# GpSimd operations of a hybrid decoder layer cut into pieces of 256 columns, and the border into the feed-forward stage regrouped

## The chip, the core and the metric

One Trainium2 chip, one of its cores. The metric is device time of one execution in microseconds (us), the median of several runs. PE is TensorE (matrix multiply; PEld is its weight load), DVE is VectorE, ACT is ScalarE, POOL is GpSimd and SP is SyncE, which issues the DMAs. SBUF is the memory on the chip from which the engines read, and PSUM the one into which TensorE writes.

## The reference

One layer, one step: a prompt of 1024 tokens and 8 single-token samples, 1024 channels, weights in float32.

```python
def layer(x, ...):
    y = mixer_block(rmsnorm(x, norm_mix_g), ...)
    x = x + y
    x = x + cross_attn(rmsnorm(x, norm_x_g), mk, mv, w_xq, w_xo)
    x = x + swiglu(rmsnorm(x, norm_ffn_g), w_gate, w_up, w_down)
...
def mixer_block(h, ...):
    proj = h @ w_in                                  # everything below is cut from proj
    rq, rk = rotary(rq, pos), rotary(rk, pos) * RET_DK ** -0.5      # 4 heads of 128
    o_r = retention_chunked(rq, rk, rv, state)       # scores, state update, chunk by chunk
    y_a = (silu(rg) * groupnorm(o_r)) @ w_branch_a
    gq, gk, gv = silu(causal_conv(qkv, 4 taps))      # 8 heads of 128
    o_g = gated_delta_chunked(l2norm(gq), l2norm(gk), gv, beta, g, state)
    y_b = (rmsnorm(o_g) * silu(z)) @ w_branch_b
    return (sigmoid(ga) * y_a + sigmoid(gb) * y_b) @ w_out
def rotary(x, pos):                                  # the rotation
    return concat([x1 * cos - x2 * sin, x1 * sin + x2 * cos])
def swiglu(h, w_gate, w_up, w_down):
    return (silu(h @ w_gate) * (h @ w_up)) @ w_down
```

## The kernel before

Every operand of a large product is split into a high part (rounded, written by ScalarE) and a low part (the rest, by one subtraction), and each product is three matmuls: high by high, high by low, low by high. `wsplit` (L245 to L255) does it for a weight tile of 128x1024: a DMA brings `wf`, ScalarE writes `wh`, and `wl = wf - wh` is written by the engine in `wlo[0]`: GpSimd in the gated-delta stage, else VectorE (L254). TensorE reads `wl` last of the three.

The stages follow each other in time, counted from the start of the span: the start (to 50 us); the gated-delta stage, in which the chains of 8 heads run beside the dense products of the input projection (50 to 950); retention, with the samples' single steps beside it (950 to about 1170); the branch products, keys and values and `w_out` (to 1490); cross-attention (to 1690); its output projection with the residual in two halves of 516 columns, the border (1690 to 1870); pairs of feed-forward column blocks (to 2260); the down projection.

On TensorE the order is written by hand in the gated-delta and retention stages; on the other engines a scheduler sets it from its own estimate of when data arrive, and each engine then works through its list in order.

In the gated-delta stage VectorE runs the four-tap convolution (`cyq`, `cyk`, `cyv`, L526, 1056 columns, both inputs in SBUF), the evacuations of the projection (`ev`, L361, input in PSUM; L365, both in SBUF) and the small steps of the recurrence (`R` L764, `S` L780). GpSimd runs `wl` (60 times) and 128x512 operations, 16 of each: `A` (L629), `dg` (L633), `qe` (L659), `U` and `Tm` (L725), `os` (L797), `ol` (L799), `oT` (L813).

In retention `ret_qk` rotates queries and keys of one unit (a head and half of the tokens, 8 units): `swapped` (L887) writes `rsw` in two operations of 64x1024 that read the other half of the partitions, then `rqk` is multiplied (L904) and added to (L905), 128x1024 each, all on GpSimd. `svn` (L1151, L1152) and `qS` (L1156, L1189) are the samples' delta-rule steps on VectorE; TensorE reads `svn`. `kv` (L1268) evacuates keys and values of the memory; TensorE waits for its bank. `b0l` to `b7l` (L236) are low parts of the gated-delta output, and `rS_0l` (L236) that of the retention state, which TensorE reads.

The border. `residual_half(c, ms)` runs `w_xo` tile by tile for token half c and adds the residual into `xr` (L1558); the squares are summed on GpSimd (L1563), and `rsnorm` (L310 to L319) turns the sum into the factor `rsB`: a logarithm (L315) and an exponential (L317) on ScalarE for each of two blocks of columns. `scale(r, c)` (L1571) multiplies 128x1032 tiles of `xr` by `rsB`; `operands(p, ...)` splits the operand of product p into `xop_0` to `xop_3`. Each pair of weight blocks (`w_gate`, `w_up`) needs seven products, as in Strassen's scheme; the sums of weights that products 5, 6, 7 and 3 need (`S1`, `S2`, `wu`) are formed on GpSimd (L1687) when `weights(p)` first asks for them, and a product (24 matmuls of 258 columns) then splits its weights into `wp_f` (L235, L236). `preload_act_table_set` puts a set of functions that holds both logarithm and exponential into ScalarE; an `ACT_TABLE_LOAD` changes the set.

Of the kernel before, what the change touches and what calls it, by code (L numbers as in the profile page):

```python
# [17 lines left out]
P = 128  # L18
# [4 lines left out]
KT = D // P  # L23
# [120 lines left out]
def build(tc, io):  # L144
# [21 lines left out]
    with ExitStack() as es:  # L166
# [73 lines left out]

        wlo = [ve]
# [379 lines left out]
        def gdn_decay(h, u):  # L621

            n = f"{h}_{u}"
            hc = slice(4 * u, 4 * u + 4)
            A = gtile("A", f"A{n}", 2)
            qe = gtile("qe", f"qe{n}", 4)
            dg = gtile("dg", f"dg{n}", 4)
            dma(out=qe, in_=gr_d[h * NCH + 4 * u:h * NCH + 4 * u + 4].rearrange("c t -> (c t)").partition_broadcast(P))
            ge.tensor_tensor(v4(A), v4(qe), bcol(gcum[:, h, hc]), op=ALU.subtract)  # L629
            se.activation(A, A, AF.Abs)  # L630
            se.activation(A, A, AF.Exp, scale=-1.0)
            se.activation(qe, qe, AF.Exp)
            ge.tensor_tensor(v4(dg), v4(A), bc(triu), op=ALU.mult)  # L633
            return qe, dg, A
# [80 lines left out]
        def gdn_inverses(h, units, U32):  # L715
# [7 lines left out]
            for u in range(2):  # L723
                for dst, src in ((Us[u], U32), (Tm[u], T32)):
                    ge.tensor_tensor(dst.rearrange("p (c b i) -> p c b i", c=4, b=4), src[:, 4 * u:4 * u + 4].unsqueeze(2).to_broadcast(sh),  # L725
                                     cst[:, C_B32:C_B32 + 4].unsqueeze(1).unsqueeze(3).to_broadcast(sh), op=ALU.mult)
# [62 lines left out]
        def gdn_outs(h):  # L789
# [5 lines left out]
            for u in n:  # L795
                se.activation(rs[u], o[u], AF.Square)
                ge.tensor_tensor(rs[u], rs[u], sqq[:, u * 512:(u + 1) * 512], op=ALU.add)  # L797
                se.activation(hi[u], rs[u], AF.Copy)
                ge.tensor_tensor(lo[u], rs[u], hi[u].bitcast(F32), op=ALU.subtract)  # L799
# [96 lines left out]
        def ret_qk(h, u):  # L896
# [505 lines left out]
        se.preload_act_table_set("natural_log_exp_and_others")  # L1402
# [187 lines left out]
        residual_half(1, range(2))  # L1590
# [6 lines left out]
        residual_half(1, range(2, KT))  # L1597
# [14 lines left out]
        stage[:] = [wp, fp, fp, fp]  # L1612
# [52 lines left out]
        class Pair:  # L1665


            def __init__(self, ft):
# [9 lines left out]
                self.at, self.seen = {}, []  # L1678
                self.t = r1tile(f"hid{ft}", F32)
# [3 lines left out]
            def weights(self, p):  # L1683
                for q in {6: (5, 6), 7: (5, 7), 5: (5,), 3: (5, 6, 3)}.get(p, ()):
# [84 lines left out]
        xt3 = [pair(r1tile, f"xt3{i}", F32) for i in range(2)]  # L1769
# [6 lines left out]
        for p, new, (r, c) in ((5, r2tile, (0, 1)), (6, r1tile, (0, 1)), (4, r1tile, (1, 0))):  # L1776
# [152 lines left out]
```

## Time and profile before

| | |
|---|---|
| runs, us | 2495.86, 2496.76, 2498.49 (median 2496.76) |
| profiled execution, us | 2501.62, its span 2499.8 |
| mean granted TensorE clock | 0.986 of full speed |
| busy, us | PE 2401.3, PEld 2314.2, DVE 1518.8, ACT 978.2, POOL 897.6 |

The profiled execution is 4.86 us longer than the median of the runs, and 1.82 us of it lie outside the span. The clock is given as a share of full speed: 1.00 is TensorE at 2.4 GHz, 0.50 is 1.2 GHz, and a value between is the mean of a stretch that has both.

### The profile page before, as it was taken

The page shows a single profiled execution, that of the slowest core. Times are in us where ns is not written, and L with a number is a line of the kernel's source. Part 1 is how long each engine was busy: PE and PEld are TensorE (multiplying, and loading weights), DVE is VectorE, ACT ScalarE, POOL GpSimd, SP SyncE. Part 2 cuts the span into 40 slices and gives each one's busy share as a digit, 9 for nine tenths or more (in the row PEclk, how much of TensorE's full clock was granted, in tenths as well). Part 3 has the DMA queues.
Part 4 walks back from the last instruction along what each step waited for, and adds up shares of the span by engine and source line. Part 5 has one row for each costly group of instructions (what it writes and reads, how often), then busy time and mean ns, then how long its engine had stood idle before and what let it go on. Part 6 is the DMA issues. An engine that isn't in the chain of part 4 may idle for free. (4 is left out here: it accounts for less than half of the span.)

```text
span 2499.8 us, 44199 instructions
## 1 busy us (share of the span) xinstructions
PE 2401.3 (96%) x17290; PEld 2314.2 (93%) x17290; DVE 1518.8 (61%) x2957; ACT 978.2 (39%) x1757; POOL 897.6 (36%) x846
## 2 busy tenths in 40 slices
PE   8999999999999999898999999998889999999998
PEld 6999999999999998788999999878889999999998
DVE  5866857668576536787544445342496656656665
ACT  4333243433424333564422343234543333335453
POOL 4344243343434327442001120003388655620233
PEclk9999999999999999999999999999989999999999
DMA  4222222222222236577666543335345445438654
GB/s 145 87 68 72 89 89 85 72 74 86 82 84 76 83 112 197 194 227 233 212 184 177 157 135 102 124 126 177 107 136 189 162 131 170 140 126 286 211 157 150
DMA packets 201090, 344.60 MB, mean 138 GB/s; under 512 B 39984, under 2 KB 125488, under 8 KB 200752
## 3 DMA queue, kind: packets, MB, share of 16 engines
q1 hardware_dynamic: 200880, 341.76, 43.5%
q8 instruction: 136, 2.23, 0.4%
q14 instruction: 74, 0.61, 0.1%
HBM read 243.91 MB, written 97.78 MB: 137 GB/s over the span
## 5 line engine op out<-in xcount | busy, mean ns | idle before, releaser
L157 PE MATMUL pd<-x0h,wh 128*128 128x344 f32 (+1 forms) x1712 | 575.9, 338 | 10.5 <-ACT x0h L238 5.5
L157 PE MATMUL pd<-x0h,wl 128*128 128x344 f32 (+1 forms) x1712 | 548.8, 322 | 0.0
L157 PE MATMUL pd<-x0l,wh 128*128 128x344 f32 (+1 forms) x1712 | 547.7, 321 | 0.4 <-DVE x0l L239 0.4
L157 PE MATMUL P<-xo,w 128*128 128x258 f32 x3696 | 453.2, 285 | 15.0 <-ACT xo L235 7.8
L157 PEld LDWEIGHTS P<-xo,w 128*128 128x128 f32 x3696 | 451.3, 192 | 16.6 <-ACT xo L235 8.4
L157 PEld LDWEIGHTS pd<-x0h,wh 128*128 128x128 f32 (+1 forms) x1712 | 323.2, 189 | 20.0 <-DVE ev L361 6.1
L157 PEld LDWEIGHTS pd<-x0l,wh 128*128 128x128 f32 (+1 forms) x1712 | 323.3, 189 | 1.9 <-DVE x0l L239 0.8
L157 PEld LDWEIGHTS pd<-x0h,wl 128*128 128x128 f32 (+1 forms) x1712 | 322.7, 189 | 1.2
L253 ACT ACTIVATE wh<-wf 128x1024 fp32r<-128x1024 f32 (+1 forms) x137 | 144.0, 1052 | 269.2 <-PE pd L157 180.9
L157 PE MATMUL D<-ho,wd 128*128 128x258 f32 x1584 | 192.3, 284 | 2.9 <-ACT ho L235 2.9
L157 PEld LDWEIGHTS D<-ho,wd 128*128 128x128 f32 x1584 | 191.8, 190 | 3.2 <-ACT ho L235 3.1
L254 POOL TENSOR_TENSOR wl<-wf,wh 128x1024 fp32r<-128x1024 f32 x60 | 144.5, 2408 | 52.0 <-ACT wh L253 51.0
L254 DVE TENSOR_TENSOR wl<-wf,wh 128x1024 fp32r<-128x1024 f32 (+1 forms) x77 | 102.7, 1333 | 54.1 <-ACT wh L253 53.8
L361 DVE TENSOR_TENSOR ev<-pd,rsB 128x344 f32<-128x344 f32 x140 | 71.1, 508 | 62.1 <-PE pd L157 56.4
L236 DVE TENSOR_TENSOR wd<-wd,wd 128x512 fp32r<-128x512 f32 (+1 forms) x96 | 67.5, 708 | 53.2 <-ACT wd L235 52.0
L706 DVE TENSOR_TENSOR tm<-Ab,px 128x16 f32<-128x16 f32 (+30 forms) x248 | 72.4, 292 | 34.7 <-POOL Ab L703 30.0
L236 DVE TENSOR_TENSOR w<-S,w 128x512 fp32r<-128x512 f32 x66 | 64.5, 977 | 41.8 <-ACT w L235 41.8
L1364 POOL TENSOR_TENSOR ma<-ma,my 128x344 f32<-128x344 f32 x24 | 22.3, 929 | 181.6 <-DVE ma L1363 166.0
L235 ACT ACTIVATE wd<-wd 128x512 fp32r<-128x512 f32 (+1 forms) x96 | 56.5, 591 | 73.5 <-PE D L157 51.9
L157 PE MATMUL pd<-oh,wh 128*128 128x258 f32 x256 | 75.2, 294 | 8.1 <-DVE xr L1558 6.0
L235 ACT ACTIVATE w<-S 128x512 fp32r<-128x512 f32 x66 | 41.6, 630 | 93.9 <-PE P L157 81.4
L157 PE MATMUL pd<-oh,wl 128*128 128x258 f32 x256 | 74.8, 293 | 2.4 <-DVE wl L254 2.4
(765 smaller groups left out, 5405.4 us busy)
## 6 DMA issues: line engine op xcount, KB each, us to landing
wf<-w_in SPq DMA_DIRECT2D x72, 512.0 KB, 3.6
wu<-w_up SPq DMA_DIRECT2D x22, 512.0 KB, 4.1
wg<-w_gate SPq DMA_DIRECT2D x22, 512.0 KB, 3.6
sd<-w_down SPq DMA_DIRECT2D x40, 256.0 KB, 4.1
wsd<-sd SPq DMA_DIRECT2D x20, 512.0 KB, 5.9
wd<-wsd SPq DMA_DIRECT2D x20, 512.0 KB, 4.2
kc<-ck SPq DMA_DIRECT2D x32, 256.0 KB, 3.8
vc<-cv SPq DMA_DIRECT2D x32, 256.0 KB, 3.5
```

The costliest lines, as they stand in the source:

```text
L157: return nc.tensor.matmul(out, lhsT=lhsT, rhs=rhs, **kw)
L235: se.activation(hi, src, AF.Copy)
L236: return ve.tensor_tensor(lo, src, hi.bitcast(F32), op=ALU.subtract)
L253: se.activation(wh[:, :kt, :m], wf, AF.Copy)
L254: wlo[0].tensor_tensor(wl[:, :kt, :m], wf, wh[:, :kt, :m].bitcast(F32), op=ALU.subtract)
L361: ve.tensor_tensor(e[:, :n], pt, rsB[:, a:b], op=ALU.mult)
L706: ve.tensor_tensor(tm[:, :, :w], Ab[:, i, :w].unsqueeze(1).to_broadcast([P, 8, w]), X[:, :, :w], op=ALU.mult)
L1364: ge.tensor_tensor(e[:, :n], e[:, :n], y[:, :n], op=ALU.add)
```

## The change

It does three things. First, a helper `pieces(n, ...)` issues one GpSimd operation as n operations on equal shares of the columns: `wl` in four of 256, the gated-delta 128x512 operations in two of 256, and the rotation of a unit goes through blocks of 256 columns, each with its two swapped products, its multiplication and its addition. Second, the preload of the table set ahead of the `w_out` residual is kept at its place in the program, where the scheduler could move it before. Third, the border: three tiles of the second half instead of two stand ahead of the first scaling; the difference `xt3` is taken of the unscaled `xr` and then scaled itself (before, `xr` was scaled and then subtracted); products 7 stand before the scalings of the second half; for the first two pairs the sums for products 5, 6 and 7 are formed when the pair is created, and the one for product 3 on VectorE; and the staging buffers of the weights take another turn.

```diff
+        def pieces(n, out, x, y, op):
+            w = out.shape[1] // n
+            for i in range(0, out.shape[1], w):
+                ge.tensor_tensor(out[:, i:i + w], x[:, i:i + w], y[:, i:i + w], op=op)
...
-            wlo[0].tensor_tensor(wl[:, :kt, :m], wf, wh[:, :kt, :m].bitcast(F32), op=ALU.subtract)
+            if wlo[0] is ge:
+                pieces(4, wl[:, :kt, :m], wf, wh[:, :kt, :m].bitcast(F32), ALU.subtract)
+            else:
+                ve.tensor_tensor(wl[:, :kt, :m], wf, wh[:, :kt, :m].bitcast(F32), op=ALU.subtract)
...
-            ge.tensor_tensor(v4(A), v4(qe), bcol(gcum[:, h, hc]), op=ALU.subtract)
+            pieces(2, v4(A), v4(qe), bcol(gcum[:, h, hc]), ALU.subtract)
...
-            rots = [rot[:, j, cs].unsqueeze(1).to_broadcast([P, 2, 512]) for j in range(2)]
-            swapped(w, qk, rots[1])
-            ge.tensor_tensor(qk, qk, rots[0], op=ALU.mult)
-            ge.tensor_tensor(qk, qk, w, op=ALU.add)
+            for j in range(2):
+                for i in range(0, 512, 256):
+                    x, y = qk[:, j, i:i + 256], w[:, j, i:i + 256]
+                    r = rot[:, :, u * 512 + i:u * 512 + i + 256]
+                    swapped(y, x, r[:, 1])
+                    ge.tensor_tensor(x, x, r[:, 0], op=ALU.mult)
+                    ge.tensor_tensor(x, x, y, op=ALU.add)
...
-        se.preload_act_table_set("natural_log_exp_and_others")
+        tc.keep_in_program_order(se.preload_act_table_set("natural_log_exp_and_others"))
...
-        residual_half(1, range(2))
+        residual_half(1, range(3))
...
-        residual_half(1, range(2, KT))
+        residual_half(1, range(3, KT))
+        xt3 = [pair(r1tile, f"xt3{i}", F32) for i in range(2)]
+        for i in range(2):
+            ve.tensor_tensor(xt3[i], xr[1][1][i], xr[0][1][i], op=ALU.subtract)
...
-        stage[:] = [wp, fp, fp, fp]
+        stage[:] = [fp, fp, fp, wp]
...
+                if ft < 2:
+                    self.sum(5, 6, 7)
...
-                        ge.tensor_tensor(o, x, y, op=op)
+                        (ve if self.ft < 2 and q == 3 else ge).tensor_tensor(o, x, y, op=op)
...
-        for i in range(2):
-            for r in (1, 0):
-                e = xr[r][1][i]
-                ve.tensor_tensor(e, e, rsB[:, half(1)].unsqueeze(1).to_broadcast([P, 2, H]), op=ALU.mult)
-            ve.tensor_tensor(xt3[i], xr[1][1][i], xr[0][1][i], op=ALU.subtract)
+        for x in xt3:
+            ve.tensor_tensor(x, x, rsB[:, half(1)].unsqueeze(1).to_broadcast([P, 2, H]), op=ALU.mult)
         operands(7, r2tile, [xt3[j // 2][:, j % 2] for j in range(4)])
+        for f in (f0, f1):
+            f.product(7)
+        scale(0, 1)
...
-        for f, p in ((f0, 7), (f1, 7), (f0, 5), (f0, 6), (f1, 6), (f0, 4), (f1, 4), (f0, 3), (f1, 5), (f1, 3)):
+        for f, p in ((f0, 3), (f1, 5), (f1, 3)):
```

(The products 5, 6 and 4 now stand in the loop over p that splits their operands; the order of the products on TensorE stays as it was.)

Three places in the instruction order. The first is GpSimd's list at the rotation of one unit in retention (`rsw` and `rqk` are the unit's tiles, `rq_1l` and `rsc_1l` the low parts of queries and scores, `exr` the samples' key operand); of before:

```order
L928 TENSOR_TENSOR rq_1l<-rqk_1_11179,rq_1h 128x512
L936 TENSOR_TENSOR rsc_1l<-rsc_1_11849,rsc_1h 128x512
L887 TENSOR_TENSOR rsw_1_11950<-rqk_1_11949,rot 64x1024 x2
L1123 TENSOR_TENSOR exr<-kq,rc 128x8x8
L904 TENSOR_TENSOR rqk_1_11949<-rqk_1_11949,rot 128x1024
L905 TENSOR_TENSOR rqk_1_11949<-rqk_1_11949,rsw_1_11950 128x1024
```

and of the change:

```order
L941 TENSOR_TENSOR rq_1l<-rqk_1_11547,rq_1h 128x512
L949 TENSOR_TENSOR rsc_1l<-rsc_1_12241,rsc_1h 128x512
L896 TENSOR_TENSOR rsw_1_12342<-rqk_1_12341,rot 64x256 x8
L917 TENSOR_TENSOR rqk_1_12341<-rqk_1_12341,rot 128x256 x2
L1136 TENSOR_TENSOR exr<-kq,rc 128x8x8
L917 TENSOR_TENSOR rqk_1_12341<-rqk_1_12341,rot 128x256 x2
L918 TENSOR_TENSOR rqk_1_12341<-rqk_1_12341,rsw_1_12342 128x256 x4
```

Four operations of 1024 columns became sixteen of 256: 8 swapped products, 4 multiplications, 4 additions, in the same place between the other operations.

The second is VectorE's list behind the norm of the border's second half (`rsB2` is the factor, `xr110` and the like the tiles to be scaled, `w2_0` the low part of the weights of product 2 of the first pair, `xo7` the operand of product 7); of before:

```order
L1773 TENSOR_TENSOR xr110_18443<-xr110_18443,rsB2_17536 128x1032
L1773 TENSOR_TENSOR xr010_18127<-xr010_18127,rsB2_17536 128x1032
L1773 TENSOR_TENSOR xr112_18588<-xr112_18588,rsB2_17536 128x1032
L1773 TENSOR_TENSOR xr012_18298<-xr012_18298,rsB2_17536 128x1032
L236 TENSOR_TENSOR w2_0_18838<-wg0_18790,w2_0_18838 128x512
L236 TENSOR_TENSOR w7_0_19012<-wu0_18791,w7_0_19012 128x512
L236 TENSOR_TENSOR w6_1_19145<-S2_1_18872,w6_1_19145 128x512
L236 TENSOR_TENSOR w4_0_19178<-wu0_18791,w4_0_19178 128x512
L1774 TENSOR_TENSOR xt30_18936<-xr110_18443,xr010_18127 128x1032
L1774 TENSOR_TENSOR xt31_18937<-xr112_18588,xr012_18298 128x1032
```

and of the change:

```order
L1791 TENSOR_TENSOR xt30_19137<-xt30_19137,rsB2_17940 128x1032
L1791 TENSOR_TENSOR xt31_19138<-xt31_19138,rsB2_17940 128x1032
L1584 TENSOR_TENSOR xr010_18531<-xr010_18531,rsB2_17940 128x1032
L1584 TENSOR_TENSOR xr012_18674<-xr012_18674,rsB2_17940 128x1032
L1584 TENSOR_TENSOR xr110_18847<-xr110_18847,rsB2_17940 128x1032
L1584 TENSOR_TENSOR xr112_18992<-xr112_18992,rsB2_17940 128x1032
L236 TENSOR_TENSOR w2_0_19249<-wg0_19198,w2_0_19249 128x512
L236 TENSOR_TENSOR w7_0_19364<-wu0_19199,w7_0_19364 128x512
L236 TENSOR_TENSOR w6_1_19525<-S2_1_19283,w6_1_19525 128x512
L236 TENSOR_TENSOR xo7_0_19352<-xt30_19137,xo7_0_19352 128x516
```

Six scalings instead of four stand ahead of `w2_0`; the two differences moved ahead of the norm.

The third is ScalarE's list at the norm of the first half (`pn` is the sum over the channels, `wh` the high part of the next `w_xo` tile); of before:

```order
L315 ACT_TABLE_LOAD
L315 ACTIVATE rsB2_17536<-pn_18119,epsc_89 128x258
L1564 ACTIVATE xr102_17974<-xr102_17974,gains_79 128x258
L317 ACT_TABLE_LOAD
L317 ACTIVATE rsB2_17536<-rsB2_17536 128x258
L315 ACT_TABLE_LOAD
L315 ACTIVATE rsB2_17536<-pn_18122,epsc_89 128x258
L1561 ACTIVATE sqx2_17535<-xr010_18127 128x258
L317 ACT_TABLE_LOAD
L317 ACTIVATE rsB2_17536<-rsB2_17536 128x258
L253 ACTIVATE wh_18301<-wf_18299 128x1024
```

and of the change:

```order
L1577 ACTIVATE xr102_18378<-xr102_18378,gains_79 128x258 x2
L324 ACTIVATE rsB2_17940<-pn_18523,epsc_89 128x258
L326 ACTIVATE rsB2_17940<-rsB2_17940 128x258
L1574 ACTIVATE sqx2_17939<-xr010_18531 128x258
L324 ACTIVATE rsB2_17940<-pn_18526,epsc_89 128x258
L326 ACTIVATE rsB2_17940<-rsB2_17940 128x258
L259 ACTIVATE wh_18677<-wf_18675 128x1024
```

The four table loads of this norm are gone. So are four at the norm of the second half and six at the norm ahead of cross-attention, and one load stands new ahead of the `w_out` residual.

## Rows read from the trace of the kernel before

**Rows 1.** Busy time by stage: from:to, length, each engine, PEclk, DMA share, GB/s.
```profile
50.00:500.00 450.00, 437.22 (x2981) 426.80 (x2980) 315.56 (x724) 160.14 (x265) 167.72 (x186) 1.00 0.27 80
500.00:950.00 450.00, 440.73 (x3017) 432.24 (x3016) 274.94 (x619) 164.00 (x276) 171.35 (x168) 1.00 0.29 90
950.00:1170.00 220.00, 197.94 (x1427) 179.90 (x1427) 169.46 (x350) 115.29 (x200) 108.91 (x77) 0.96 0.63 206
...
1690.00:1870.00 180.00, 154.20 (x1138) 149.70 (x1138) 101.79 (x144) 88.70 (x164) 86.32 (x63) 0.91 0.45 132
1870.00:2260.00 390.00, 389.71 (x3252) 389.51 (x3250) 240.27 (x414) 126.30 (x254) 219.89 (x190) 1.00 0.48 155
```

**Rows 2.** Timeline of GpSimd, VectorE and TensorE, gated-delta stage.
```profile
84.62 2.39 POOL L254 TENSOR_TENSOR wl<-wf,wh 128x1024 fp32r<-128x1024 f32 x1
...
85.65 2.47 DVE L526 SCALAR_TENSOR_TENSOR cyq<-preq,cw,cyq 128x1056 f32<-128x1056 f32 x1
...
88.16 1.32 DVE L526 SCALAR_TENSOR_TENSOR cyq<-preq,cw,cyq 128x1056 f32<-128x1056 f32 x1
...
89.96 0.43 PE L157 MATMUL pd<-x0h,wh 128*128 128x344 f32 x1 [2.25 <-DVE ev L361]
...
95.05 0.32 PE L157 MATMUL pd<-x0h,wl 128*128 128x344 f32 x1
```

**Rows 3.** TensorE's waits, gated-delta stage: us in total, times, longest.
```profile
PE pv L157 <- DVE R L764: 7.4, 9, 1.4
```

**Rows 4.** Groups of GpSimd by form: count, busy us, mean ns, idle before.
```profile
L254 POOL TENSOR_TENSOR wl<-wf,wh 128x1024 fp32r<-128x1024 f32 x60 | 144.5, 2408 | 52.0 <-ACT wh L253 51.0
...
L1657 POOL TENSOR_TENSOR sd<-sd 128x256 f32<-128x256 f32 x20 | 16.0, 800 | 18.5 <-DMA sd<-w_down 18.4
```

**Rows 5.** TensorE's waits, retention stage (950 to 1170 us).
```profile
PE pks L157 <- DVE svn L1152: 6.1, 2, 3.9
PE pro L161 <- DVE kv L1268: 5.8, 1, 5.8
PE pro L157 <- DVE rS_0l L236: 4.5, 2, 3.4
```

**Rows 6.** Timeline of VectorE and GpSimd in retention, from 1030 us on.
```profile
1030.11 0.27 DVE L1152 TENSOR_SCALAR svn<-svn,bs 8x128 f32<-8x128 f32 x1
...
1055.57 4.91 POOL L887 TENSOR_TENSOR rsw<-rqk,rot 64x1024 f32<-64x1024 f32 x2
...
1058.21 2.36 DVE L1152 TENSOR_SCALAR svn<-svn,bs 8x128 f32<-8x128 f32 x1
...
1125.68 3.36 DVE L236 TENSOR_TENSOR b3l<-bf,b3h 128x1024 fp32r<-128x1024 f32 x1
```

**Rows 7.** Timeline of ScalarE at the norm of the border's first half.
```profile
1737.32 1.28 ACT L315 ACT_TABLE_LOAD   x1
1738.62 0.48 ACT L315 ACTIVATE rsB<-pn,epsc 128x258 f32<-128x258 f32 x1
...
1744.63 0.42 ACT L317 ACTIVATE rsB<-rsB 128x258 f32<-128x258 f32 x1
```

**Rows 8.** VectorE and TensorE behind that norm (timeline), and the stretch that follows.
```profile
1745.08 2.38 DVE L1571 TENSOR_TENSOR xr<-xr,rsB 128x1032 f32<-128x1032 f32 x2 [6.18 <-ACT rsB L317]
...
1747.85 0.58 PE L157 MATMUL pd<-oh,wh 128*128 128x258 f32 x1 [5.68 <-DVE xr L1558]
...
1747.20:1754.00 6.80, 6.15 (x28) 6.16 (x29) 2.65 (x6) 1.41 (x4) 0.74 (x1) 0.50 0.51 155
```

**Rows 9.** Timeline of VectorE, GpSimd and TensorE behind the border's second norm.
```profile
1804.77 4.67 DVE L1773 TENSOR_TENSOR xr<-xr,rsB 128x1032 f32<-128x1032 f32 x4 [6.62 <-ACT rsB L317]
1809.35 0.69 DVE L236 TENSOR_TENSOR w<-wg,w 128x512 fp32r<-128x512 f32 x1
...
1811.32 18.09 POOL L1687 TENSOR_TENSOR S<-wg,S 128x512 f32<-128x512 f32 x1 [14.84 <-DVE w L236]
...
1834.00 18.72 PE L157 MATMUL P<-xo,w 128*128 128x258 f32 x133 [4.91 <-ACT xo L235]
```

More of the change, by code (lines that the diff above doesn't have):

```diff
@@ L632, in gdn_decay @@
             se.activation(qe, qe, AF.Exp)
-            ge.tensor_tensor(v4(dg), v4(A), bc(triu), op=ALU.mult)
+            pieces(2, v4(dg), v4(A), bc(triu), ALU.mult)
             return qe, dg, A
@@ L658, in gdn_qk @@
             sl = lambda t, c: t[:, u * 512 + c * P:u * 512 + (c + 1) * P]
-            ge.tensor_tensor(qe, q[:, u * 512:u * 512 + 512], qe, op=ALU.mult)
+            pieces(2, qe, q[:, u * 512:u * 512 + 512], qe, ALU.mult)
             pt = (pi if u else pf)("pqk")
@@ L724, in gdn_inverses @@
                 for dst, src in ((Us[u], U32), (Tm[u], T32)):
-                    ge.tensor_tensor(dst.rearrange("p (c b i) -> p c b i", c=4, b=4), src[:, 4 * u:4 * u + 4].unsqueeze(2).to_broadcast(sh),
-                                     cst[:, C_B32:C_B32 + 4].unsqueeze(1).unsqueeze(3).to_broadcast(sh), op=ALU.mult)
+                    pieces(2, dst.rearrange("p (c b i) -> p c b i", c=4, b=4), src[:, 4 * u:4 * u + 4].unsqueeze(2).to_broadcast(sh),
+                           cst[:, C_B32:C_B32 + 4].unsqueeze(1).unsqueeze(3).to_broadcast(sh), ALU.mult)
             yield 8.0
@@ L796, in gdn_outs @@
                 se.activation(rs[u], o[u], AF.Square)
-                ge.tensor_tensor(rs[u], rs[u], sqq[:, u * 512:(u + 1) * 512], op=ALU.add)
+                pieces(2, rs[u], rs[u], sqq[:, u * 512:(u + 1) * 512], ALU.add)
                 se.activation(hi[u], rs[u], AF.Copy)
-                ge.tensor_tensor(lo[u], rs[u], hi[u].bitcast(F32), op=ALU.subtract)
+                pieces(2, lo[u], rs[u], hi[u].bitcast(F32), ALU.subtract)
             yield 9.0
@@ L812, in gdn_outs @@
                 dma(out=z, in_=zd[h][:, u * 512:(u + 1) * 512])
-                ge.tensor_tensor(o[u], o[u], z, op=ALU.mult)
+                pieces(2, o[u], o[u], z, ALU.mult)
                 dma(out=bd[h][:, u * 512:(u + 1) * 512], in_=o[u])
@@ L1681, in __init__, with sum, weights @@
                 self.U = [up.tile([P, BLK], F32, name=f"U{ft}_{i}", tag="ev" if ft % 2 else "gt")[:, :H // 2] for i in range(2)]
-            def weights(self, p):
-                for q in {6: (5, 6), 7: (5, 7), 5: (5,), 3: (5, 6, 3)}.get(p, ()):
+            def sum(self, *qs):
+                for q in qs:
                     if q in self.sums:
                         o, x, y, op = self.sums.pop(q)
-                        ge.tensor_tensor(o, x, y, op=op)
+                        (ve if self.ft < 2 and q == 3 else ge).tensor_tensor(o, x, y, op=op)
+            def weights(self, p):
+                self.sum(*{6: (5, 6), 7: (5, 7), 5: (5,), 3: (5, 6, 3)}.get(p, ()))
                 w = wop(f"w{p}_{self.ft}")
@@ L1768, in build @@
             f1.product(p)
-        xt3 = [pair(r1tile, f"xt3{i}", F32) for i in range(2)]
-        for i in range(2):
-            for r in (1, 0):
-                e = xr[r][1][i]
-                ve.tensor_tensor(e, e, rsB[:, half(1)].unsqueeze(1).to_broadcast([P, 2, H]), op=ALU.mult)
-            ve.tensor_tensor(xt3[i], xr[1][1][i], xr[0][1][i], op=ALU.subtract)
+        for x in xt3:
+            ve.tensor_tensor(x, x, rsB[:, half(1)].unsqueeze(1).to_broadcast([P, 2, H]), op=ALU.mult)
         operands(7, r2tile, [xt3[j // 2][:, j % 2] for j in range(4)])
-        for p, new, (r, c) in ((5, r2tile, (0, 1)), (6, r1tile, (0, 1)), (4, r1tile, (1, 0))):
+        for f in (f0, f1):
+            f.product(7)
+        scale(0, 1)
+        for p, new, (r, c), fs in ((5, r2tile, (0, 1), [f0]), (6, r1tile, (0, 1), [f0, f1]), (4, r1tile, (1, 0), [f0, f1])):
             for i in range(2):
@@ L1780, in build @@
             operands(p, new, quarters(r, c))
+            if p == 5:
+                scale(1, 1)
+            for f in fs:
+                f.product(p)
         operands(3, r1tile, quarters(1, 1))
-        for f, p in ((f0, 7), (f1, 7), (f0, 5), (f0, 6), (f1, 6), (f0, 4), (f1, 4), (f0, 3), (f1, 5), (f1, 3)):
+        for f, p in ((f0, 3), (f1, 5), (f1, 3)):
             f.product(p)
```

## The prediction

> **What bounds the kernel now.** I read busy time by stage first [rows 1]. From 1870 to 2260 us TensorE is busy 389.71 of 390 us, with 3252 matmuls, 0.12 us each: there nothing but fewer matmuls would help, and the change removes none. What can be won lies where TensorE stands still or runs at the lower clock: 12.78 + 9.27 = 22.1 us idle in the gated-delta stage (50 to 950), 22.1 us idle in retention (950 to 1170) and 25.8 us idle in the border (1690 to 1870). Retention's mean clock of 0.96 costs (1 - 0.96) x 220 = 8.8 us more, the border's 0.91 costs 0.09 x 180 = 16.2 us. Together that is 95 us, the pot from which every term below comes.
>
> Then I asked in each stage what ends TensorE's waits. In the gated-delta stage it is VectorE's small steps, `R` first, 7.4 us in nine waits [rows 3]; in retention VectorE's `svn`, `kv` and `rS_0l`, 6.1, 5.8 and 4.5 us [rows 5]; in the border the norm's factor and what VectorE and GpSimd make behind it [rows 8, 9]. So the question is why VectorE is late while it is busy 57 to 77% of these stages.
>
> The timeline answers. `cyq` that starts 1.0 us into a GpSimd `wl` takes 2.47 us, and the next alike, with GpSimd free, 1.32; the `wl` itself (84.62 + 2.39 = 87.01) ends 1.1 us before the long `cyq` does [rows 2]. The operation stood until GpSimd was done and then ran. TensorE's next matmul came 2.25 us late, behind `ev`, which stands after these on VectorE [rows 2]. In retention `svn` takes 0.27 us alone and 2.36 us under `rsw` of the rotation, and `b3l`, 1024 columns, 3.36 us [rows 6]. VectorE's operations with both inputs in SBUF wait for the whole GpSimd operation under way.
>
> **Gated-delta pieces.** Added are 60 x 3 instructions for `wl` and 16 x 1 for each of eight 128x512 sites; no bytes. A piece costs GpSimd between 2408 / 4 = 0.60 us and the 0.80 us that 128x256 takes in the feed-forward stage [rows 4]. So GpSimd gains at most 60 x 4 x 0.8 - 144.5 = 47 us of work on the wl's and is then about 43% busy instead of 38% [rows 1]. That lies beside TensorE: a `wl` that ends at 87.01 is first read at 95.05 [rows 2], 8 us of slack, and a piece held up by three convolution taps would be 3 x 1.32 = 4 us late. Cost zero; it would start where the slack is gone.
>
> The gain: a blocked VectorE operation now waits at most one piece, 0.6 to 0.8 us, not up to 2.4. About half of the stage's 22.1 us idle stands behind a VectorE operation that was just blocked so, as at 89.96; the other half behind the recurrence itself. Of the 11 us I take half, 5, since a run of VectorE operations meets the later pieces one by one. Bounds: 0 (it meets all four) and 11.
>
> **Rotation pieces.** Four operations of about 2.46 us (4.91 for two `rsw` [rows 6]) become sixteen of 0.6 to 0.8, 10 to 13 us a unit on GpSimd, as before; by the program TensorE reads them a unit later. Blocked operations here stand right on the path: `svn` and `rS_0l` are read by TensorE, and `kv` stands behind `b3l` on VectorE. Waits behind these three are 16.4 us of the 22.1 idle [rows 5]. Of the 2.1 us by which `svn` was held at most 0.7 stays, so two thirds of the 16.4 go; I take 10, since some of it is not the rotation's. Each of these long waits is followed by half clock, as 1747.20 to 1754 is behind a 5.68 us wait [rows 8]; shorter waits, such as the 2.25 at 89.96, left the stage at 1.00 [rows 1, 2]. Of the 8.8 us I take half, 4. Term: 14. Bounds: 3 (only `kv`'s wait halves) and 22 (all idle but 9 us, and the whole clock).
>
> The Trainium skill says under "SBUF — State Buffer", Who interferes with whom, that the port pair these two engines share is an exclusive lock held for a whole instruction, and that the loser fully blocks. The long `cyq` and `svn` agree [rows 2, 6]. Taken strictly it also speaks against the change: cutting leaves the total time under lock as it was, which is the first rival below, 2480 instead of 2464.
>
> **Border, first half.** ScalarE's norm runs from 1737.32 to 1745.05 with four table loads of 1.28 us in it, each followed at once by its function (1737.32 + 1.28 = 1738.60, start 1738.62) [rows 7]. Without them it ends at 1739.9. Behind it VectorE scales for 2.38 us at 1745.08, and only then evacuates the bank for which TensorE waits 5.68 us at 1747.85 [rows 8]. The loads take 5.1 off that wait. The rest, 0.6, is too short to cost the clock, and the 6.80 us at 0.50 behind it, worth 3.4 us, goes too: 8.5 us. I take 8; bounds 5 (the clock falls all the same) and 8.5. The six loads at the cross-attention norm and the new one I cost at nothing: that stretch is not in the pot above.
>
> The same skill, "ScalarE: Activation LUTs", What ACT_TABLE_LOAD costs, gives an estimate of 2.66 us a switch with a drain. The rows show no drain [rows 7]; by the page the eight loads on the border's path would be 21 us, by the rows 10, and the border's terms 11 us larger.
>
> **Border, second half.** VectorE starts its four scalings at 1804.77 for the same chain [rows 9], so without loads at 1799.65. But six scalings of 1.15 us stand there now: they end at 1806.5 instead of 1809.35, 2.85 us earlier. That is the lower bound. The upper: before, GpSimd's sum `S` for product 3 took 18.09 us, since VectorE ran two-input operations back to back; ScalarE's conversion of it stood in line ahead of an `xo`, and TensorE waited 4.91 us until 1834.00 [rows 9]. That sum is now VectorE's. Up to the first `xo6` its new list has 19 operations of 512 or 516 columns (0.60 us, the step from 1809.35), 5 more of 1.15 and 2 evacuations of about 0.35: 17.9 us, so 1824.4 instead of 1834.00, 9.6 earlier. Between, I take 6: nearer neither end, since GpSimd's sums of the third pair still block VectorE there and half clock is likely to appear again behind a wait for `w2_0`.
>
> **Sum.** 5 + 14 + 8 + 6 = 33 us. The profiled execution lasted 2501.62 us (span 2499.8 and 1.82 outside); it would be 2468.6. The runs' median lies 4.86 lower, so I predict 2496.76 - 33 = 2463.8, rounded 2464. The bounds add to 0 + 3 + 5 + 2.9 = 11 and 11 + 22 + 8.5 + 9.6 = 51.
>
> **Rivals.**
> *Alternation.* VectorE's queue is full wherever it matters, so the four pieces block four operations instead of one, and TensorE gets its operand as late as before. For: at 1055.57 two `rsw` in a row blocked two operations. Against: most of VectorE's list, evacuations, reads PSUM and passes. Then pieces give 3 us, the border 14: 2480.
> *The border takes its gain back.* Six scalings ahead of `w2_0`, then VectorE's list as bound, with half clock behind each wait: the second half gives 0, the first 5: 19 + 5 = 24, so 2473.
> *All of it.* Half clock vanishes in retention and border: toward 51, about 45: 2452.
> *Starved pieces (slower).* GpSimd loses against a VectorE that runs back to back, as `S` did for 18.09 us [rows 9], at each of the sixteen pieces; `rq` and `rsc` low parts stand behind the rotation on GpSimd, and TensorE reads them in each of 8 units. With 5 + 14 won elsewhere (gated-delta, border), TensorE must wait 2.4 us a unit longer for the kernel to be no faster; at 4 us it is 32 - 19 = 13 slower, 2510. Against: in retention VectorE is busy 77% and mostly in evacuations [rows 1].
> *No change in what the engines do:* excluded by the order.
>
> **Chances.** Forecast as summed (2456 to 2472) 0.60, alternation 0.16, border gives back 0.10, all of it 0.08, starved pieces 0.06. A difference under 0.2%, 5 us, can't be told from no change. Starved pieces mild end there: same 0.03, slower 0.04, faster 0.93. The range from 2447 (50 us) to 2486 (11 us) leaves out the slow rival and the outer edges; the likeliest case's own range is 2456 to 2472.
>
> **What will show it.** `cyq`'s long form near 2.0 or less instead of 2.47; `svn` under 1 us; GpSimd pieces at 0.6 to 0.8; no table load at the border's norms; TensorE's wait before the second half's next `w_xo` tile under 1 us and its clock 1.00 there; no 18 us `S`; retention's clock above 0.98. It is wrong if TensorE's waits in retention stay near 22 us under other names (alternation), if waits on GpSimd's `rsc` or `rqk` appear (starved), or if the stretch behind the second norm keeps its waits at half clock.

## The result, and the profile after

The changed kernel takes 2463.51 us (median of 4 runs, 2461.29 to 2466.83) against 2497.62 us for the kernel before (median of 4 runs): ratio 0.9865, 95% interval 0.9851 to 0.9879. The forecast was 2464, so 33 us less; 34 were measured. The profiled execution lasted 2466.83 us with a span of 2465.0, the slowest of the four.

Busy time on the page of the changed kernel:

```profile
PE 2393.1 (97%) x17290; PEld 2306.1 (94%) x17290; DVE 1466.0 (59%) x2961; ACT 962.2 (39%) x1744; POOL 992.8 (40%) x1248
```

VectorE has 4 instructions more than before and is busy 52.8 us less; GpSimd, with two sums fewer to form (those for product 3), is busy 95 us more. Time in which an operation stands blocked counts as busy here, as the long `cyq` of [rows 2] shows, so part of the blocking moved from VectorE to GpSimd.

By stage (columns as in [rows 1]), each stretch bounded by the same matmuls in both traces: from 50 us to retention's first matmul `pkq`, and from there to the first of the memory's keys. Of the kernel before:

```profile
50.00:944.78 894.78, 872.73 (x5960) 853.83 (x5958) 586.28 (x1336) 321.62 (x537) 334.00 (x351) 1.00 0.28 85
944.78:1143.03 198.25, 176.19 (x1269) 160.58 (x1266) 154.50 (x315) 101.77 (x180) 111.08 (x76) 0.96 0.63 203
```

and of the changed kernel, with the border's window of [rows 1] moved up by the 30.7 us that were won by the feed-forward's first matmul:

```profile
50.00:929.82 879.82, 867.98 (x5943) 851.27 (x5942) 543.01 (x1335) 320.97 (x537) 428.80 (x655) 1.00 0.28 86
929.82:1119.67 189.85, 178.83 (x1268) 162.28 (x1266) 136.43 (x315) 102.44 (x181) 132.62 (x169) 0.96 0.65 216
...
1659.26:1839.26 180.00, 158.82 (x1208) 151.65 (x1208) 110.82 (x154) 81.74 (x161) 71.89 (x65) 0.94 0.50 152
```

TensorE's idle time (length less its busy time) fell from 22.1 to 11.8 us in the gated-delta stage, from 22.1 to 11.0 in retention and from 25.8 to 21.2 in the border. Its clock in retention did not rise: 0.96 in both traces.

The stretch of [rows 2] in the changed kernel, as a timeline (GpSimd, VectorE, TensorE):

```profile
81.05 4.85 POOL L245 TENSOR_TENSOR wl<-wf,wh 128x256 fp32r<-128x256 f32 x4
...
82.08 1.52 DVE L535 SCALAR_TENSOR_TENSOR cyq<-preq,cw,cyq 128x1056 f32<-128x1056 f32 x1
...
83.64 1.67 DVE L535 SCALAR_TENSOR_TENSOR cyq<-preq,cw,cyq 128x1056 f32<-128x1056 f32 x1
...
85.79 0.42 PE L157 MATMUL pd<-x0h,wh 128*128 128x344 f32 x1 [0.68 <-DVE ev L370]
```

The convolution that took 2.47 us takes 1.52, the next 1.67 instead of 1.32, and TensorE's wait fell from 2.25 to 0.68 us. The price stands on GpSimd: four pieces last 4.85 us where the whole lasted 2.39, because now GpSimd waits for VectorE between pieces. A mean piece costs 0.95 us, not the 0.60 to 0.80 that [rows 4] bounded; half of the 240 pieces take 0.74 us or less, so some of the price is the cutting itself and the rest is waiting:

```profile
L245 POOL TENSOR_TENSOR wl<-wf,wh 128x256 fp32r<-128x256 f32 x240 | 219.9, 949 | 46.4 <-ACT wh L259 45.0
L896 POOL TENSOR_TENSOR rsw<-rqk,rot 64x256 f32<-64x256 f32 x64 | 51.8, 810 | 8.9 <-DMA rqk<-rqkd 5.3
```

No wait of TensorE in this stage names the weights' part, so the 8 us of slack bore it.

Retention, TensorE's waits of the changed kernel (as [rows 5]) and one `svn` under the rotation's pieces (as [rows 6]):

```profile
PE prs L157 <- POOL rqk L918: 2.7, 1, 2.7
PE pro L161 <- DVE kv L1281: 2.5, 1, 2.5
...
PE pks L157 <- DVE svn L1165: 1.0, 2, 0.6
...
1043.06 5.25 POOL L896 TENSOR_TENSOR rsw<-rqk,rot 64x256 f32<-64x256 f32 x6
...
1044.06 0.74 DVE L1165 TENSOR_SCALAR svn<-svn,bs 8x128 f32<-8x128 f32 x1
```

`svn` fell from 2.36 to 0.74 us, TensorE's wait for it from 6.1 to 1.0 and for `kv` from 5.8 to 2.5. In the first row stands a new one: TensorE waits for the rotated queries of the first unit, at 939.60 us.

The border's first half (as [rows 7, 8]): ScalarE, VectorE, TensorE, and the stretch around.

```profile
1713.08 0.46 ACT L324 ACTIVATE rsB<-pn,epsc 128x258 f32<-128x258 f32 x1
...
1714.82 0.42 ACT L326 ACTIVATE rsB<-rsB 128x258 f32<-128x258 f32 x1
...
1715.27 2.38 DVE L1584 TENSOR_TENSOR xr<-xr,rsB 128x1032 f32<-128x1032 f32 x2 [1.30 <-ACT rsB L326]
...
1718.04 0.39 PE L157 MATMUL pd<-oh,wh 128*128 128x258 f32 x1 [0.52 <-DVE xr L1571]
...
1715.00:1722.00 7.00, 6.49 (x55) 6.27 (x54) 4.70 (x6) 3.10 (x7) 0.75 (x1) 1.00 0.59 160
```

The chain lasts 2.2 us instead of 7.7, the wait is 0.52 instead of 5.68 (0.6 was forecast), and the clock stays at 1.00.

The second half (as [rows 9]): VectorE, one of GpSimd's sums for the next pair, then TensorE.

```profile
1766.63 2.38 DVE L1791 TENSOR_TENSOR xt<-xt,rsB 128x1032 f32<-128x1032 f32 x2 [0.32 <-ACT rsB L326]
1768.92 4.66 DVE L1584 TENSOR_TENSOR xr<-xr,rsB 128x1032 f32<-128x1032 f32 x4
...
1786.24 4.55 DVE L1799 TENSOR_TENSOR xr<-xr,xr 128x1032 f32<-128x1032 f32 x2
...
1794.35 1.76 DVE L236 TENSOR_TENSOR xo<-xr,xo 128x516 fp32r<-128x516 f32 x1
...
1787.55 2.14 POOL L1705 TENSOR_TENSOR wu<-wg,wu 128x512 f32<-128x512 f32 x1
...
1774.24 13.52 PE L157 MATMUL P<-xo,w 128*128 128x258 f32 x90 [3.23 <-DVE w L236]
...
1796.16 2.52 PE L157 MATMUL P<-xo,w 128*128 128x258 f32 x10 [6.37 <-DVE xo L236]
```

The 18 us sum is gone, and yet TensorE waits 3.23 us for `w2_0` and 6.37 us for the first `xo6`. VectorE works from 1766.63 with one gap of 0.70 us, at 1785.63, where it waits for ScalarE; two differences take 4.55 us instead of 2.3 and the first low part of `xo6` 1.76 instead of 0.6, beside GpSimd's sums for the next pair.

The start times of five matmuls in the two traces:

| first matmul of | before | after | won by then |
|---|---|---|---|
| retention's setup (`pkq`, behind the gated-delta stage) | 944.78 | 929.82 | 14.96 |
| the memory's keys (`pd<-mh,wh`) | 1143.03 | 1119.67 | 23.36 |
| cross-attention (`pd<-x1h,wh`) | 1489.02 | 1465.91 | 23.11 |
| feed-forward (`P`) | 1791.13 | 1760.38 | 30.75 |
| down projection (`D`) | 2262.62 | 2228.15 | 34.47 |

By this table the gated-delta stage and the start won 15 us, retention 8.4, the border and what precedes it 11.4, where 5, 14 and 14 were forecast: a right sum of three wrong terms. But it compares one execution with one other, and these lie above the medians of their kernels, by 4.9 us (before) and 3.3 us (changed). The experiments ask whether it is so.

### The profile page after: what moved, and what is told of

It is laid out like the page before. It is cut to its first block, busy times and chain, and to the rows that moved or that the text cites. A ratio compares the mean times of both kernels' runs of the same rounds, so it can differ in the third digit from the quotient of the medians.

```text
span 2465.0 us, 44666 instructions
## 1 busy us (share of the span) xinstructions
PE 2393.1 (97%) x17290; PEld 2306.1 (94%) x17290; DVE 1466.0 (59%) x2961; ACT 962.2 (39%) x1744; POOL 992.8 (40%) x1248
## 4 chain that ended last, share of the span: by engine, by line
PE 78%; DVE 7%; DMA 7%; ACT 3%; issue 2%; POOL 1%; SPq 1%; DVEq 0%; ACTq 0%; POOLq 0%
PE pd L157 40%; PE P L157 17%; PE D L157 7%; PE pl L157 1%; DMA Ab<-scr 1%; PE E L157 1%; DMA xs<-x1d 1%; PE psc L157 1%; PE ppv L157 1%; DMA wf<-w_xo 1%; PE pot L157 1%; PE pro L157 1%; PE pov L157 1%; DMA af<-ad 1%; ACT wh L259 1%
## 5 line engine op out<-in xcount | busy, mean ns | idle before, releaser
L245 POOL TENSOR_TENSOR wl<-wf,wh 128x256 fp32r<-128x256 f32 x240 | 219.9, 949 | 46.4 <-ACT wh L259 45.0
L716 DVE TENSOR_REDUCE px<-tm 128x8 f32<-128x16 f32 (+30 forms) x248 | 73.8, 298 | 5.0
```

Of the source, the lines that this page charges most:

```text
L245: ge.tensor_tensor(out[:, i:i + w], x[:, i:i + w], y[:, i:i + w], op=op)
L716: ve.tensor_reduce(X[:, :, i], tm[:, :, :w], axis=AX.X, op=ALU.add, negate=True)
```

## The experiments

Each kernel was compared with the kernel before on its own chip; the median of before lay between 2494.25 and 2497.62 us, so kernels of different chips are compared by ratios. 0.1% is 2.5 us.

| kernel | us, median | ratio to before | 95% interval |
|---|---|---|---|
| changed | 2463.51 | 0.9865 | 0.9851 to 0.9879 |
| changed, weights' part whole | 2470.01 | 0.9897 | 0.9878 to 0.9915 |
| changed, rotation whole | 2475.40 | 0.9924 | 0.9904 to 0.9944 |
| changed, preload free | 2473.81 | 0.9914 | 0.9897 to 0.9931 |
| changed, border of before | 2462.42 | 0.9869 | 0.9852 to 0.9887 |
| changed, 512-column operations whole | 2463.41 | 0.9868 | 0.9852 to 0.9885 |
| changed, weights' part in eight | 2461.92 | 0.9864 | 0.9846 to 0.9882 |
| border of before, sum 3 on VectorE | 2463.95 | 0.9868 | 0.9851 to 0.9885 |
| before, preload held | 2484.39 | 0.9957 | 0.9942 to 0.9973 |
| before, rotation in pieces | 2477.91 | 0.9931 | 0.9917 to 0.9944 |
| before, weights' part in pieces | 2488.65 | 0.9975 | 0.9966 to 0.9985 |
| changed, first unit's rotation whole | 2458.78 | 0.9847 | 0.9830 to 0.9863 |
| changed, first unit partly on VectorE | 2455.24 | 0.9841 | 0.9825 to 0.9857 |

**The weights' part whole** in the changed kernel.

```diff
-                pieces(4, wl[:, :kt, :m], wf, wh[:, :kt, :m].bitcast(F32), ALU.subtract)
+                pieces(1, wl[:, :kt, :m], wf, wh[:, :kt, :m].bitcast(F32), ALU.subtract)
```

> The changed kernel with the weights' low part in one GpSimd operation of 1024 columns again; all else as changed. Length theory (VectorE waits for the rest of one GpSimd instruction, so its length counts): most of the 15 us gained up to the end of the gated-delta stage goes, about 11 of them, so about 2474 us, and the long convolution operation is back at 2.47 us. Alternation theory (only the total time under lock counts): 2463 to 2466, with TensorE's waits in the gated-delta stage as in the changed kernel.

6.5 us slower than the changed kernel by the medians, 0.32% by the ratios, whose intervals touch. All four runs (2466.14 to 2471.91) lie above the alternation's 2463 to 2466; the length theory's 11 us were too many. The kernel with the border of before, which is as fast as the changed one (below), took 2460.31 to 2465.65 on the same chip. What VectorE's convolution shows, mean ns of `cyk` in the gated-delta stage, first in the kernel before, then with the weights' part whole, in four and in eight pieces:

```profile
L526 DVE SCALAR_TENSOR_TENSOR cyk<-prek,cw,cyk 128x1056 f32<-128x1056 f32 x24 | 43.1, 1794 | 8.0 <-ACT cyk L524 7.8
```

```profile
L535 DVE SCALAR_TENSOR_TENSOR cyk<-prek,cw,cyk 128x1056 f32<-128x1056 f32 x24 | 40.5, 1688 | 7.9 <-ACT cyk L533 7.7
```

```profile
L535 DVE SCALAR_TENSOR_TENSOR cyk<-prek,cw,cyk 128x1056 f32<-128x1056 f32 x24 | 36.4, 1518 | 7.8 <-ACT cyk L533 7.6
```

```profile
L535 DVE SCALAR_TENSOR_TENSOR cyk<-prek,cw,cyk 128x1056 f32<-128x1056 f32 x24 | 35.0, 1458 | 7.7 <-ACT cyk L533 7.4
```

1.79, 1.69, 1.52, 1.46 us against 1.30 alone: the shorter GpSimd's instruction, the shorter the wait. If four pieces together held up VectorE for as long as the whole had, the mean would not fall. In part the alternation is real: the median of the 24 rises from 1.32 us before to 1.52 in the changed kernel, so more operations are held up, but the longest falls from 2.50 to 1.80.

**The rotation whole** in the changed kernel (the four operations of the kernel before in place of the loop).

> The changed kernel with the rotation of a unit in four operations of 1024 columns again. Length theory with the term of the prediction: 14 us slower, 2477 us. Length theory with what the changed kernel's trace shows (the first unit's rotation ends later in pieces and holds TensorE 2.7 us, so 5 to 9 us are given back at the stage's start): net 8 us slower, 2472 us. Alternation: 2462 to 2465, and the wait of TensorE for the first unit's rotation is gone.

12 us slower (0.59% by the ratios, 15 us): the prediction's term of 14, not the 8 that the changed kernel's trace seemed to show.

**The preload free** in the changed kernel.

```diff
-        tc.keep_in_program_order(se.preload_act_table_set("natural_log_exp_and_others"))
+        se.preload_act_table_set("natural_log_exp_and_others")
```

> The changed kernel without holding the preload of the table set at its place. If the table loads make the norms of the border late: fourteen loads are back, four in each of the border's norms, 5.1 us in each chain; first half 7 us, second half 1 to 5 us given back, so about 2473 us. If the border is bound by VectorE's and TensorE's work anyway: 2464 to 2467 us.

10.3 us slower. By matmul starts, this kernel wins 1.9 us from cross-attention's start to the feed-forward's start and loses 1.1 us in the feed-forward, where the changed kernel wins 7.6 and 3.7: 5.8 and 4.8 us, about one norm's table loads (5.1 us) in each half. In this kernel, as in every trace without the held preload, TensorE waits 5.7 to 5.9 us behind the first norm; in none of the traces with it.

**The border's order of before** in the changed kernel, with the preload held (`residual_half(1, range(2))`, the scalings and differences behind the norm, all sums on GpSimd when asked for).

> The changed kernel with the border's order of before (and the preload kept). If the first half's gain is the table loads and the second half's is the regrouping: 2 to 4 us slower, 2466 to 2468 us, with an 18 us sum on GpSimd again. If the six scalings ahead of the first low part of weights cost what the regrouping saves: within 1 us of the changed kernel, 2463 to 2464 us.

1.1 us faster by the medians and 0.04% slower by the ratios, which is no difference: the regrouping brings nothing that can be told. Its GpSimd sum and TensorE's wait:

```profile
1773.56 17.45 POOL L1700 TENSOR_TENSOR S<-wg,S 128x512 f32<-128x512 f32 x1 [9.29 <-DVE w L236]
...
1796.19 20.76 PE L157 MATMUL P<-xo,w 128*128 128x258 f32 x148 [7.63 <-ACT xo L235]
```

TensorE goes on at 1796.19, behind the long sum, 37.2 us after its first feed-forward matmul (1758.95); in the changed kernel at 1796.16, behind VectorE's list, 35.8 us after it (1760.38).

**The eight 512-column operations whole** in the changed kernel (`pieces(2, ...)` becomes `pieces(1, ...)`).

> The changed kernel with the eight gated-delta operations of 512 columns whole again; the weights' low part stays in pieces of 256. Length theory: these operations hold VectorE for at most 1.3 us, half as long as the weights' part did, and there are 128 of them against 60; undoing the weights' pieces cost 6.5 us, so undoing these should cost about half of it or more, 3 to 6 us: 2467 to 2469 us. Rival (only the operation that was longest mattered, since these run where VectorE has no work with two SBUF inputs): 2463 to 2465 us.

No difference in time, as the rival has it. But the rival's reason, that VectorE has nothing there to be held up, does not hold. In its trace `cyk` takes 1.63 us on average where the changed kernel has 1.52. The stretch from 50 us to retention's first matmul with the weights' part alone in pieces (below, the kernel `before, weights' part in pieces`), then this kernel's, then this kernel's retention:

```profile
50.00:935.39 885.39, 867.57 (x5947) 850.27 (x5947) 557.26 (x1335) 320.88 (x537) 403.64 (x525) 1.00 0.28 86
```

```profile
50.00:937.42 887.42, 869.80 (x5961) 852.46 (x5960) 558.62 (x1336) 320.72 (x537) 403.15 (x529) 1.00 0.28 85
937.42:1117.84 180.42, 171.19 (x1268) 155.79 (x1266) 134.06 (x315) 101.78 (x180) 129.35 (x163) 1.00 0.68 223
```

TensorE is idle for 17.8 and 17.6 us in the gated-delta stage when only the weights' part is in pieces, 17.3 when only the eight operations are (the weights' part whole), 22.1 with neither and 11.8 with both (in the other traces 21.6 and 23.1 with neither, 11.9 to 14.4 with both). So the eight operations cost TensorE as many waits as the weights' part, about 5 us. What they win there does not reach the end in these traces: with them whole the stage ends 7.6 us later than in the changed kernel, but retention takes 180.4 us at a clock of 1.00 instead of 189.9 at 0.96, and the memory's keys begin 1.8 us earlier. Why retention takes the gain back is not shown; each of these lengths is read from one execution.

**The weights' part in eight pieces** (`pieces(8, ...)`).

> The changed kernel with the weights' low part in eight pieces of 128 columns. Length theory: what a blocked VectorE operation waits falls from about 0.6 to 0.35 us; undoing the pieces from 256 to 1024 columns cost 6.5 us, so 128 gives at most 1 to 2 us more: 2461 to 2463 us. Rival (each piece costs GpSimd and VectorE a handover, so more pieces are worse): VectorE's busy time rises above the changed kernel's 1466 us and the time with it, 2466 us or more.

No difference that can be told, within the length theory's bounds. VectorE is busy 10 us less than in the changed kernel, GpSimd 58 us more.

**Only sum 3 on VectorE**, with the border of before.

```diff
-                        ge.tensor_tensor(o, x, y, op=op)
+                        (ve if self.ft < 2 and q == 3 else ge).tensor_tensor(o, x, y, op=op)
```

> The changed kernel with the border's order of before, and only the two sums for product 3 on VectorE instead of GpSimd. With the old border TensorE waited 7.6 us behind a GpSimd sum that lasted 17 us. If that starved sum is the border's wait: 3 to 6 us faster than the changed kernel, 2458 to 2461 us, and no long sum. If VectorE's own list is as late (it gets two operations of 0.6 us more): 2462 to 2464 us, with a wait of about 6 us for an operand from VectorE in its place.

No faster: the second theory holds in its time, not in its wait of about 6 us. The wait behind the long sum became several shorter ones, most of them behind VectorE's list (TensorE's waits, 1680 to 1850 us):

```profile
PE P L157 <- DVE xo L236: 3.4, 3, 2.3
...
PE P L157 <- DVE U L1732: 2.6, 1, 2.6
```

**Each part alone in the kernel before**: the preload held, the rotation in pieces, the weights' part in pieces (edits as in the diff of the change).

> The kernel before with one line changed: the preload of the table set held at its place. Undoing it in the changed kernel cost 10.3 us. If its gain stands by itself: 10 us under the kernel before. If it needs the rest of the change (the border's VectorE list as bound): 4 to 7 us under it.

> The kernel before with only the rotation in pieces of 256 columns, the first unit too. Undoing it in the changed kernel cost 12 us; the prediction's term was 14. Length theory: 10 to 14 us under the kernel before. Alternation: within 3 us of it. If the retention stage only makes up for what the gated-delta stage left it (its end was nearly the same in kernels whose gated-delta stages ended up to 7 us apart): 14 us or more.

> The kernel before with only the weights' low part in four pieces. Undoing it in the changed kernel cost 6.5 us, the prediction's term for the whole gated-delta stage was 5. If the gain stands by itself: 5 to 7 us under the kernel before. If the retention stage behind it takes it back (its rotation still whole, its end bound by its own waits): 0 to 3 us.

The ratios say 0.43%, 0.69% and 0.25% less: 10.7, 17.2 and 6.2 us of 2497, each known to 2 to 4 us by its interval. Their sum, 34.1 us, is the whole change's 34, and the two parts left out of it, the eight operations and the regrouping, measured nothing when undone. The parts stand by themselves, and in the kernel with the weights' part alone its gain is not taken back.

The preload alone also shows where the second norm's table loads cost time. Of the kernel before, ScalarE and TensorE at that norm, where TensorE needs the bank that `U` (L1717) empties, and `U` stands on ScalarE behind three of the four loads; then TensorE's first 60 us of the feed-forward, in the kernel before:

```profile
1802.63 0.38 ACT L1717 ACTIVATE U<-P 128x258 f32<-128x258 f32 x1
...
1803.06 6.08 PE L157 MATMUL P<-xo,w 128*128 128x258 f32 x28 [4.02 <-ACT U L1717]
...
1791.13:1851.13 60.00, 46.49 (x308) 45.09 (x308) 46.87 (x58) 32.89 (x61) 38.56 (x19) 0.83 0.25 75
```

with the preload held and nothing else changed, where the GpSimd sum and the wait behind it are still there:

```profile
1792.43 18.08 POOL L1687 TENSOR_TENSOR S<-wg,S 128x512 f32<-128x512 f32 x1 [9.29 <-DVE w L236]
...
1815.09 18.73 PE L157 MATMUL P<-xo,w 128*128 128x258 f32 x133 [4.87 <-ACT xo L235]
...
1778.51:1838.51 60.00, 48.82 (x346) 47.29 (x347) 53.14 (x70) 28.81 (x60) 42.46 (x21) 0.89 0.25 80
```

and in the changed kernel:

```profile
1760.38:1820.38 60.00, 46.76 (x321) 44.65 (x322) 56.78 (x72) 28.48 (x58) 24.64 (x19) 0.83 0.25 78
```

The wait of 4.02 us behind `U` is gone wherever the preload is held. In 60 us TensorE runs 308 matmuls before, 346 with the preload alone and 321 with the regrouping as well, where its clock is again 0.83 as before.

**The first unit's rotation whole**, the other seven in pieces; then **its multiplication and addition on VectorE** as well.

```diff
+            if h + u == 0:
+                rots = [rot[:, j, cs].unsqueeze(1).to_broadcast([P, 2, 512]) for j in range(2)]
+                swapped(w, qk, rots[1])
+                ge.tensor_tensor(qk, qk, rots[0], op=ALU.mult)   # ve in the second kernel
+                ge.tensor_tensor(qk, qk, w, op=ALU.add)          # ve in the second kernel
+                return qk
```

> The changed kernel with the rotation of the first unit alone in four whole operations; the other seven in pieces. If the pieces of the first unit end later than the whole operations and TensorE waits for that (2.7 us in the changed kernel's trace, and the stretch behind it at half clock): that wait is gone, 2 to 5 us faster, 2459 to 2461 us. If the wait only moves to what stands behind it (the next unit or the samples' operands): 2463 to 2465 us.

> The changed kernel with the first unit's rotation whole, and its multiplication and addition on VectorE instead of GpSimd (the swapped products stay on GpSimd). With the first unit's rotation whole on GpSimd the time was 2458.8 us and TensorE still waited 1.3 us for it. If that wait is the stage's start: 1 to 3 us less than that, 2456 to 2458 us, and no wait for the rotated queries. If VectorE's evacuations behind the two long operations become late instead: 2459 to 2462 us.

4.7 us and 8.3 us faster than the changed kernel by the medians (0.18% and 0.24% by the ratios, 4.5 and 6.0 us), by the medians just past what was expected of them; the interval of the first overlaps the changed kernel's, that of the second by its edge, so the first alone is not clear of the noise. GpSimd at the first unit in the kernel before, 10.7 us from 940.10 to 950.80:

```profile
940.10 4.85 POOL L887 TENSOR_TENSOR rsw<-rqk,rot 64x1024 f32<-64x1024 f32 x2 [0.86 <-DMA rqk<-rqkd]
945.03 2.42 POOL L904 TENSOR_TENSOR rqk<-rqk,rot 128x1024 f32<-128x1024 f32 x1
947.52 3.28 POOL L905 TENSOR_TENSOR rqk<-rqk,rsw 128x1024 f32<-128x1024 f32 x1
```

and in the changed kernel, 13.0 us from 927.25 to 940.23, with TensorE's wait and two stretches of its clock:

```profile
927.25 7.36 POOL L896 TENSOR_TENSOR rsw<-rqk,rot 64x256 f32<-64x256 f32 x8 [0.85 <-DMA rqk<-rqkd]
934.68 2.81 POOL L917 TENSOR_TENSOR rqk<-rqk,rot 128x256 f32<-128x256 f32 x4
937.45 2.78 POOL L918 TENSOR_TENSOR rqk<-rqk,rsw 128x256 f32<-128x256 f32 x4
...
939.60 1.91 PE L157 MATMUL prs<-rqk 128*128 128x128 f32 x8 [2.74 <-POOL rqk L918]
...
930.00:945.00 15.00, 12.26 (x74) 11.67 (x74) 5.95 (x11) 4.93 (x9) 14.38 (x19) 0.89 0.63 211
...
980.00:990.00 10.00, 10.00 (x55) 9.54 (x53) 6.76 (x24) 2.02 (x4) 6.97 (x10) 0.78 0.49 175
```

With VectorE's help the same stretches are

```profile
930.00:945.00 15.00, 13.60 (x94) 12.75 (x92) 8.52 (x15) 5.46 (x9) 10.37 (x12) 1.00 0.67 219
...
980.00:990.00 10.00, 10.00 (x93) 8.81 (x92) 6.83 (x22) 6.05 (x12) 5.63 (x11) 1.00 0.81 289
```

and the wait for `rqk` is gone. 2455.24 us is the fastest version that was run.

## Why the prediction was right, and where not

**What bounds.** Right: TensorE's waits behind blocked VectorE operations and the border's norms were the pot. Waits fell where they were read.

**Gated-delta pieces, 5 us, bounds 0 to 11.** Right in size by time: 6.2 us alone, 6.5 when undone, both of the weights' part. The other eight sites, counted in the same sentence, changed no time, though TensorE's idle time in the stage says that they remove as many waits: both together took away 10 of its 22 us, near the upper bound, and in the traces what the eight sites won there was lost again in retention. Cost zero on GpSimd was right in this stage although a piece took 0.95 us and not 0.60 to 0.80.

**Rotation pieces, 14 us, bounds 3 to 22.** Right in size: 17 alone, 12 to 15 when undone. Of its two parts the waits, 10, came as forecast: retention's idle time fell by 11 us in the changed kernel. The clock, 4, did not come there (0.96 in both traces, where above 0.98 was named as the sign); with the rotation alone in pieces it did:

```profile
939.99:1121.02 181.03, 172.56 (x1268) 156.68 (x1266) 134.24 (x315) 101.64 (x180) 130.72 (x165) 0.99 0.68 223
```

There the idle time is 8.5 us and the stage 17.2 us shorter than before. The sentence that TensorE reads the rotation a unit later was wrong for the first unit, whose queries are read at once. There the wait on GpSimd's `rqk` appeared that was named as a sign of the starved pieces, in one unit of eight. Treating that unit apart won 4.7 and 8.3 us by the medians, 4.5 and 6.0 by the ratios.

**Border, first half, 8 us.** Right in mechanism: the chain without loads, the wait of 0.5 us, the clock. In size it is nearer the lower bound of 5. The matmul starts give 7.6 from cross-attention's start to the feed-forward's (302.1 us before, 294.5 after), but the same stretch takes 298.6 and 298.9 us in the two other kernels of the old border, and 293.5 with the preload alone: 5 to 6 us from the loads, the rest from what the one trace of the kernel before has besides.

**Border, second half, 6 us, bounds 2.85 to 9.6.** This term came out near its size for another reason. From the feed-forward's first matmul to the down projection's it is 471.50 us before, 467.77 after and 465.18 with the preload alone: the half won 3.7 us, the loads by themselves 6.3 (4.8 when undone), and the regrouping, from which the distance to 9.6 was taken, nothing. Two steps failed. The lower bound led the loads through VectorE's scalings alone and so gave them 2.85; they also held up ScalarE's `U`, for which TensorE waited 4.02 us, and that wait went with them. And "so 1824.4 instead of 1834.00" took the new VectorE list at its free durations, 24.8 us from the factor to the first `xo6`; it lasted 29.5 (1766.63 to 1796.16), with operations in it held beside GpSimd's sums (3.4 us in three of them) and a wait of 0.7 for ScalarE, and so ended about where the long sum had ended, 29.2 us behind the factor. The sign of being wrong that was named for this half, waits at half clock behind the second norm, was met: the clock of the 60 us there is 0.83 before and after. Taking the sum away from the old border alone did not help either.

**Sum.** 5 + 14 + 8 + 6 = 33 against 34.1 from the three parts alone: rotation 3 more, weights 1 more, border 3 to 4 less. That it came within 1 us is luck, since the terms missed by up to 4 us each way and are known no better than that; it came right in part by offset, but less so than the table of matmul starts made it look. The table loads on the border's path were worth 10 to 11 us, the sum of their rows, and not the 21 of the other estimate that the prediction gives; the six at the cross-attention norm, costed at nothing, were worth nothing (from the memory's keys to cross-attention 346.0 us before, 346.2 after).

**Alternation.** Refuted in time, where it gave 2480, and in its claim that VectorE is held up as long as before: VectorE's busy time fell by 52.8 us, and a convolution's mean fell with the length of GpSimd's instruction. The rule of the Trainium skill ("SBUF — State Buffer", Who interferes with whom) that the lock is held for one instruction agrees with this reading; the conclusion that cutting changes nothing does not follow from it, since the waiting engine enters between two pieces: in the changed kernel two convolutions of 1.52 and 1.67 us run within the 4.85 us of four pieces.

**Left open.** Why the gated-delta and retention stages of single executions differ by several us between kernels that are the same there was not settled. The clock in retention is part of it: 0.96 in the changed kernel, 0.99 with the rotation alone and 1.00 with the eight operations whole, though the rotation is in the same pieces in all three. TensorE's wait for the first unit's rotation goes along with it, 2.7, 0.8 and 1.0 us.

## What to carry to other kernels

Cut a GpSimd operation with SBUF inputs where VectorE's operations beside it, with two inputs in SBUF, are waited for and its own result has slack; leave it whole (or give part of it to VectorE) where its own result is next on the path. Before regrouping a stage, add up the list of the engine that will bind afterwards with the durations that it has beside the other engines, not its free ones. Judge a part by undoing it and by running it alone; the length of a stage moved by several us from trace to trace here, so bound a stage by the same instructions in both traces, and look at more than two.

## What the runs showed of the hardware

Pieces of 256 columns took GpSimd 0.95 us each beside a busy VectorE, so the 60 weights' parts cost it 219.9 us instead of 144.5; eight pieces raised its busy time by 58 us more, and the kernel took the same time. An activation table load took 1.28 us with its function right behind it. Holding one line of the program in place, which removed 14 loads and added one, was worth 10 us.
